# Three summed pairs instead of two in each gate/up block of a hybrid decoder layer

## The chip, the cores and the metric

One Trainium2 chip, one core of it. The metric is the device time in microseconds (us) of one execution of the whole layer, as a median of several runs. Engines are named as in the profile: PE is the matrix engine (PEld its weight loads), DVE the vector engine, ACT the scalar engine, POOL GpSimd, SP the engine that issues the weight transfers.

## The reference, cut to what matters

```
h = x + concat(lru, retention)(rmsnorm(x)) @ w_out        # 256 tokens, model width 2048
u = rmsnorm(h, ln2_w)
ff = silu(u @ w_ffn_gate) * (u @ w_ffn_up)                 # 2048 -> 5632, twice
h = h + ff @ w_ffn_down                                    # 5632 -> 2048
out = rmsnorm(h, final_norm_w)
```

All arrays are float32. The change touches the line of `ff`: the two products of the 256x2048 activations with the 2048x5632 gate and up weights.

## The kernel before

Every large product is made of matmuls on numbers split in two: a float32 tile is cast to a shorter format by ACT (`wh`, line 101) and the remainder is a subtraction on DVE (`wl`, line 102). A product of two split operands is three matmuls: high by high, high by low, low by high (lines 664, 665, 666).

The gate and up products run in 11 blocks of 512 columns (`ffn_block`). In a block the two token halves and the two matrices form a 2x2 array of results: c11 and c21 are the gate columns for tokens 0-127 and 128-255, c12 and c22 the up columns. Each result is 128x512 and stays in a PSUM bank of the pool `paux` (4 banks) while the 2048 rows of the weights go by as 8 *pairs* of 128-row tiles (one `Quad` each, numbered 0 to 7). A pair is a 2x2 by 2x2 block product. Most pairs do it with the 8 plain products (`EIGHT`); a *summed* pair does it with 7 (`SEVEN`), a Strassen-like scheme that multiplies sums of operands. The weights' sums t1 to t4 are built on DVE (lines 625, 626, 628, 629) from the raw 128x512 quarters, and then split like any weight; the activations' sums s1 to s4 are built once for all blocks (`Left`, lines 529 to 535). Four of the seven products (p1, p5, p6, p7) accumulate over all summed pairs of a block in four PSUM banks of their own (pool `pmm`, 4 banks); when the last summed pair is done DVE turns them into contributions to c11, c12, c21, c22 (lines 723 to 729), and at the end of the block lines 731 and 733 add these to what `paux` holds. `gated` then makes silu(gate)*up for each token half (lines 707 to 709).

A summed pair loads as two 512 KB transfers like any other, but takes more tiles: b11 is split alone (`bh`, `bl`, 128x512), then t1|t2, t3|t4 and b22|b21 are split as 128x1024 tiles. So it takes three of the four `wh`/`wl` tile pairs in rotation (pool `split`) and four of the five `raw` tiles (two loaded, two `sum`), where a plain pair takes two and two.

When a block is over, its gated result is transposed for the down product: `turn(b)` (lines 711 to 718) makes four 128x128 transposes on PE into a bank of `pmm` (`ft`), which ACT copies out. The turns are deferred by a number of steps, a step being one pair: turn(0) after the next block's pair 0, turn(1) after its pair 1.

The order of instructions on each engine is fixed when the kernel is built, by a scheduler that starts from the program order; on the chip every engine runs its list in that order and waits for what it needs. Down projection blocks (`down_block`) follow the gate/up blocks and use the same pair scheme, with summed pairs 2, 5, 8, 11, 14 of 22.

Of the kernel before, what the change touches and what calls it, by code (L numbers as in the profile page):

```python
# [28 lines left out]

SUMMED = (2, 4)
SUMMED_DOWN = (2, 5, 8, 11, 14)


# [1 line left out]
def tile_hymba_layer(ctx: ExitStack, tc: tile.TileContext, A: dict, out: bass.AP):  # L37
# [21 lines left out]
    def act_tile(name, dt=F32):  # L59
        return apool.tile([P, 512], dt, tag="act", name=nm(name))  # L60
# [7 lines left out]
    def bank(name):  # L68
        return pmm.tile([P, 512], F32, tag="mm", name=nm(name))
# [149 lines left out]
    def defer(steps, f):  # L219
        later.append([steps, f])  # L220
# [321 lines left out]
    def out_post(f, ps):  # L542
# [10 lines left out]
        if f % 2:  # L553
            hh[f // 2] = Left(hf[0], f // 2 in SUMMED)
        sq = sumsq[:, :S] if f == 0 else act_tile("sq")[:, :S]
# [7 lines left out]
    def norm2():  # L563

        ps = bank("rms")
        for t in range(2):
            pe.matmul(ps[:, 2 * t : 2 * t + 2], sumsq[:, t * P : t * P + P], ones[:, 0:2], start=True, stop=True)
        rsqrt_small(r2_tok, ps[:, 0:4:2], 1.0 / D, 2)
        v.tensor_scalar(out=r2_half, in0=r2_tok, scalar1=0.5, scalar2=None, op0=ALU.mult)
        v.tensor_tensor(out=r2_sq, in0=r2_half, in1=r2_tok, op=ALU.mult)  # L570
# [3 lines left out]
    def resid_tok(cb):  # L574
        for t in range(2):
            ps = bank("ht")
            for i in range(4):
                pe.transpose(ps[:, i * P : i * P + P], xs(4 * cb + i)[:, t * P : t * P + P], ident)
            htok[(cb, t)] = xpool.tile([P, 512], F32, tag="xh", name=nm("htok"))
            act.copy(out=htok[(cb, t)], in_=ps)  # L580
# [61 lines left out]
    def block(quads, lefts, post, ps, tail=(), after=None, ordered=False):  # L642


        n = len(quads) - (2 if tail else 0)
        todo = [(i, c, a, b, 0, 512) for i, q in enumerate(quads[:n]) for c, a, b in (SEVEN if q.sums else EIGHT)]
        for c, c0, cw in tail:
            todo += [(n, c, a, b, c0, cw, i) for i in range(n, len(quads)) for o, a, b in EIGHT if o == c[:3]]
        firsts, lasts = {}, {}
        for m, (_, c, *_) in enumerate(todo):  # L650
            firsts.setdefault(c, m)
            lasts[c] = m
        at = [0]

        def step(i):
            def run():
                while at[0] < len(todo) and todo[at[0]][0] == i:
                    m, (_, c, a, b, c0, cw, *q) = at[0], todo[at[0]]
                    if firsts[c] == m:
                        ps[c] = (aux if c in ("c11", "c12", "c21", "c22") else bank)(c)  # L660
                    q = q[0] if q else i
                    (ah, al), (bh, bl) = lefts[q][a], (t[:, c0 : c0 + cw] for t in quads[q].parts[b])
                    p, last = ps[c][:, c0 : c0 + cw], lasts[c] == m
                    pe.matmul(p, ah, bh, start=firsts[c] == m, stop=False)  # L664
                    pe.matmul(p, ah, bl, start=False, stop=False)  # L665
                    pe.matmul(p, al, bh, start=False, stop=last)  # L666
                    if last:
                        post(c)
                    at[0] += 1
                if after:  # L670
                    after(i)

            return run

        for i in range(n):
            program.append(([quads[i]], step(i)))
        if tail:

            def end():
                with tc.manual_schedule(engines={nc.tensor.engine}) if ordered else ExitStack():  # L680
                    step(n)()

            program.append((quads[n:], end))

    def ffn_block(j):
        def after(i):
            if j == 0 and i == SUMMED[-1] + 1:
                norm2()
            if j in (1, 2) and i < 2:
                resid_tok(2 * j - 2 + i)  # L690
            if j == NB - 1 and i == 0:
                load_fw()

        ps = {}
        quads = [Quad(A["w_gu"][j * (KT // 2) + i], i in SUMMED) for i in range(KT // 2)]
        block(quads, hh, ffn_post(j, ps), ps, after=after)

    def ffn_post(j, ps):
        part = {}

        def other(c, name, a, b, op=ALU.subtract):
            part[c] = act_tile(name)
            v.tensor_tensor(out=part[c], in0=a, in1=b, op=op)

        def gated(t):
            g, u, th = part["c21" if t else "c11"], part["c22" if t else "c12"], act_tile("th")
            act.activation(out=th, in_=g, func=AF.Tanh, scale=r2_half[:, t : t + 1])
            v.scalar_tensor_tensor(out=g, in0=th, scalar=1.0, in1=g, op0=ALU.add, op1=ALU.mult)
            v.scalar_tensor_tensor(out=g, in0=u, scalar=r2_sq[:, t : t + 1], in1=g, op0=ALU.mult, op1=ALU.mult)

        def turn(b):
            pt = bank("ft")
            for c in range(2):
                for t, g in enumerate((part["c11"], part["c21"])):
                    o = c * S + t * P
                    pe.transpose(pt[:, o : o + P], g[:, (2 * b + c) * P : (2 * b + c) * P + P], ident)  # L716
            ff[2 * j + b] = act_tile("ff")
            act.copy(out=ff[2 * j + b], in_=pt)

        def post(c):  # L720
            if c == "p1":
                part["c11"] = act_tile("c11")
                act.copy(out=part["c11"], in_=ps[c])
            elif c == "p7":
                n = act_tile("n")
                v.tensor_tensor(out=n, in0=ps["p6"], in1=part["c11"], op=ALU.subtract)
                other("c12", "c12", n, ps["p5"])
                other("c21", "c21", n, ps["p7"])
                other("c22", "c22", part["c21"], ps["p5"])
            elif c in ("c11", "c12", "c22"):  # L730
                v.tensor_tensor(out=part[c], in0=ps[c], in1=part[c], op=ALU.add)
            elif c == "c21":
                v.tensor_tensor(out=part[c], in0=ps[c], in1=part[c], op=ALU.subtract)
            if c == "c12":
                gated(0)
            if c == "c22":
                gated(1)
                defer(2, lambda: turn(0))
                defer(3, lambda: turn(1))

        return post

# [3 lines left out]
    def load_fw():  # L746
        for c in range(4):
            fw[c] = late_tile("fw")
            nc.sync.dma_start(out=fw[c], in_=A["final_norm_w"][c * 512 : c * 512 + 512].partition_broadcast(P))
# [199 lines left out]
    for step, (units, run) in enumerate(program):  # L949
        need += 2 * len(units)  # L950
        while done < min(len(loads), need + AHEAD):
            un, j = loads[done]
# [108 lines left out]
```

## Time and profile before

| what | value |
|---|---|
| median of 3 runs | 1109.3 us (1109.11 to 1110.9) |
| profiled execution | 1109.8 us, of which the span from first to last instruction is 1108.0 us |
| gate/up blocks | from 387.7 us to about 865 us, 43.12 us each where nothing else runs beside them |
| down blocks | from about 865 us to the end |

The profile is of one execution. The page gives busy time by engine, the share of each in 40 slices of the span, and the chain of work that ended last; the trace behind it is asked for instructions in order of time, for groups by line, and for who waited for whom. A duration of a matmul (0.39 us) is longer than the distance at which the next one starts, since matmuls overlap; the same holds for DVE, with a smaller overlap.

### The profile page before, as it was taken

How to read it: one execution, taken by the hardware profiler on the slowest of the kernel's cores; microseconds unless marked ns; L12 is line 12 of the kernel's file. 1: busy time of each engine (PE TensorE's matmuls, PEld its weight loads, DVE VectorE, ACT ScalarE, POOL GpSimd, SP SyncE). 2: the span in 40 equal slices, each digit the busy share in tenths (PEclk: the TensorE clock that was granted, in tenths of full speed). 3: DMA queues.
4: the chain of work that ended last, by engine and by line, in shares of the span. 5: the costliest groups of instructions: out<-in, count | busy, mean ns of one | idle time of the engine just before them, and what ended most of it. 6: DMA issues, size and time to landing. Idle time of an engine off the chain costs nothing.

```text
span 1108.0 us, 15102 instructions
## 1 busy us (share of the span) xinstructions
PE 1096.1 (99%) x5584; PEld 934.8 (84%) x5584; DVE 880.4 (79%) x1233; ACT 617.2 (56%) x830; POOL 57.7 (5%) x64
## 2 busy tenths in 40 slices
PE   9999999999999999999999999999999999999996
PEld 7998888889988988888888888888888888888885
DVE  7797799987766787787877877887887999777774
ACT  7666644468555565554545545545545666554553
POOL 0602230000000000000000000000000000020001
PEclk9999999999999999999999999999999999999998
DMA  9754575554565555645746656556457465646572
GB/s 323 242 190 153 172 251 168 171 182 150 194 217 188 174 182 177 231 131 192 237 143 228 208 172 228 169 195 226 143 201 243 155 206 199 226 161 212 200 240 76
DMA packets 62217, 214.74 MB, mean 194 GB/s; under 512 B 7104, under 2 KB 7488, under 8 KB 62144
## 3 DMA queue, kind: packets, MB, share of 16 engines
q1 hardware_dynamic: 61344, 211.70, 56.8%
q0 software_dynamic: 512, 1.57, 0.4%
q8 instruction: 43, 0.70, 0.3%
q10 hardware_dynamic: 288, 0.52, 0.1%
q14 instruction: 30, 0.25, 0.1%
HBM read 211.67 MB, written 2.10 MB: 193 GB/s over the span
## 4 chain that ended last, share of the span: by engine, by line
PE 95%; DMA 2%; ACT 1%; POOL 1%; DVE 1%; issue 0%; SPq 0%; DVEq 0%; ACTq 0%; POOLq 0%
PE c L665 18%; PE c L664 18%; PE c L666 18%; PE fm L140 10%; PE fm L141 5%; PE fm L146 3%; PE fm L147 3%; PE fm L145 3%; PE p L666 3%; PE p L664 3%; PE p L665 3%; PE tm L157 2%; PE tm L158 2%; PE tm L156 2%; DMA x<-in_x 1%; PE ft L716 1%
## 5 line engine op out<-in xcount | busy, mean ns | idle before, releaser
L102 DVE TENSOR_TENSOR wl<-raw,wh 128x1024 fp32r<-128x1024 f32 (+1 forms) x364 | 437.3, 1214 | 159.4 <-ACT wh L101 157.8
L101 ACT CAST wh<-raw 128x1024 fp32r<-128x1024 f32 (+1 forms) x364 | 371.2, 1032 | 293.2 <-PE c L666 145.2
L665 PE MATMUL c<-wl,ah 128*128 128x512 f32 x848 | 326.5, 391 | 0.0
L666 PE MATMUL c<-wh,al 128*128 128x512 f32 x848 | 325.5, 389 | 0.0
L664 PE MATMUL c<-wh,ah 128*128 128x512 f32 x848 | 286.5, 390 | 0.0
L666 PEld LDWEIGHTS c<-wh,al 128*128 128x128 f32 x848 | 159.3, 188 | 32.6
L665 PEld LDWEIGHTS c<-wl,ah 128*128 128x128 f32 x848 | 159.2, 188 | 32.7
L664 PEld LDWEIGHTS c<-wh,ah 128*128 128x128 f32 x848 | 159.1, 188 | 32.8
L101 ACT CAST wh<-sum 128x1024 fp32r<-128x1024 f32 x64 | 66.9, 1053 | 85.1 <-PE c L666 40.1
L140 PE MATMUL fm<-u,wh 128*128 128x512 f32 x256 | 90.7, 398 | 0.0
L102 DVE TENSOR_TENSOR wl<-sum,wh 128x1024 fp32r<-128x1024 f32 x64 | 76.8, 1219 | 3.1 <-ACT wh L101 2.5
L140 PE MATMUL fm<-y,wh 128*128 128x512 f32 x224 | 78.9, 398 | 0.0
L146 PE MATMUL fm<-u,wh 128*128 128x256 f32 x256 | 72.7, 284 | 0.0
L145 PE MATMUL fm<-u,wh 128*128 128x256 f32 x256 | 72.7, 284 | 0.0
L147 PE MATMUL fm<-u,wl 128*128 128x256 f32 x256 | 72.3, 283 | 0.0
L141 PE MATMUL fm<-u,wl 128*128 128x256 f32 x256 | 71.9, 281 | 0.0
L141 PE MATMUL fm<-y,wl 128*128 128x256 f32 x224 | 62.4, 281 | 0.0
L820 POOL TENSOR_TENSOR htok<-htok,fw 128x512 f32<-128x512 f32 (+1 forms) x7 | 10.9, 1577 | 906.2 <-ACT junk L818 906.2
L140 PEld LDWEIGHTS fm<-u,wh 128*128 128x128 f32 x256 | 48.1, 188 | 11.6
L140 PEld LDWEIGHTS fm<-y,wh 128*128 128x128 f32 x224 | 41.9, 188 | 10.2
L146 PEld LDWEIGHTS fm<-u,wh 128*128 128x128 f32 x256 | 49.1, 192 | 0.1
L145 PEld LDWEIGHTS fm<-u,wh 128*128 128x128 f32 x256 | 49.1, 192 | 0.1
(248 smaller groups left out, 1497.6 us busy)
## 6 DMA issues: line engine op xcount, KB each, us to landing
raw<-in_w_gu SPq DMA_DIRECT2D x176, 512.0 KB, 5.0
raw<-in_w_down SPq DMA_DIRECT2D x88, 512.0 KB, 4.5
raw<-in_w_out SPq DMA_DIRECT2D x32, 512.0 KB, 4.3
raw<-in_w_lx SPq DMA_DIRECT2D x16, 512.0 KB, 4.9
raw<-in_w_k SPq DMA_DIRECT2D x16, 512.0 KB, 3.7
raw<-in_w_q SPq DMA_DIRECT2D x16, 512.0 KB, 4.3
raw<-in_w_rg SPq DMA_DIRECT2D x16, 512.0 KB, 3.7
raw<-in_w_lg SPq DMA_DIRECT2D x16, 512.0 KB, 3.6
```

Source lines behind the costliest of these rows:

```text
L101: act.copy(out=dst_h, in_=src)
L102: v.tensor_tensor(out=dst_l, in0=src, in1=dst_h.bitcast(F32), op=ALU.subtract)
L140: pe.matmul(ps, wh, hl, start=first, stop=False)
L141: pe.matmul(ps[:, :S], wl, hl[:, :S], start=False, stop=last)
L145: pe.matmul(ps, wh, hl[:, :S], start=first, stop=False)
L146: pe.matmul(ps, wh, hl[:, S:], start=False, stop=False)
L147: pe.matmul(ps, wl, hl[:, :S], start=False, stop=last)
L156: pe.matmul(ps, ah, wh, start=first, stop=False)
L157: pe.matmul(ps, ah, wl, start=False, stop=False)
L664: pe.matmul(p, ah, bh, start=firsts[c] == m, stop=False)
L665: pe.matmul(p, ah, bl, start=False, stop=False)
L666: pe.matmul(p, al, bh, start=False, stop=last)
```

## The change

The first line gives three summed pairs (1, 3, 5) in each gate/up block in place of two (2, 4). The second keeps `norm2` (the second norm's factors, in block 0 alone) where it was, after pair 5. The third puts turn(1) behind pair 0 of the next block, beside turn(0): the four banks of `pmm` are taken by p1, p5, p6, p7 from pair 1 on.

```
-SUMMED = (2, 4)
+SUMMED = (1, 3, 5)
...
-            if j == 0 and i == SUMMED[-1] + 1:
+            if j == 0 and i == SUMMED[-1]:
                 norm2()
...
                 gated(1)
                 defer(2, lambda: turn(0))
-                defer(3, lambda: turn(1))
+                defer(2, lambda: turn(1))
```

What this does to the lists of instructions is shown at three places. A number at the end of a name tells tiles of one kind apart; the two kernels number them differently.

**The end of a block.** First DVE, from the first of the four additions that end a block (L731 and L733) to the first `gated` result (L709 on c11, written 1252 here and 1297 below). Before:

```order
L731 TENSOR_TENSOR c_1252_6383<-c_1204_6189,c_1252_6383 128x512
L733 TENSOR_TENSOR c_1255_6398<-c_1205_6196,c_1255_6398 128x512
L625 TENSOR_TENSOR sum_6580<-raw_6537 128x512
L731 TENSOR_TENSOR c_1254_6396<-c_1206_6203,c_1254_6396 128x512
L708 SCALAR_TENSOR_TENSOR c_1252_6383<-th_6516,c_1252_6383 128x512
L626 TENSOR_TENSOR sum_6580<-sum_6580,raw_6578 128x512
L708 SCALAR_TENSOR_TENSOR c_1255_6398<-th_6527,c_1255_6398 128x512
L731 TENSOR_TENSOR c_1256_6400<-c_1207_6210,c_1256_6400 128x512
L102 TENSOR_TENSOR bl_6540<-raw_6537,bh_6539 128x512
L709 SCALAR_TENSOR_TENSOR c_1252_6383<-c_1254_6396,r_sq,c_1252_6383 128x512
```

With the change, at the same place:

```order
L731 TENSOR_TENSOR c_1297_6494<-c_1243_6267,c_1297_6494 128x512
L733 TENSOR_TENSOR c_1300_6509<-c_1244_6274,c_1300_6509 128x512
L731 TENSOR_TENSOR c_1299_6507<-c_1245_6281,c_1299_6507 128x512
L731 TENSOR_TENSOR c_1301_6511<-c_1246_6288,c_1301_6511 128x512
L102 TENSOR_TENSOR wl_6613<-sum_6608,wh_6612 128x1024
L102 TENSOR_TENSOR wl_6619<-sum_6609,wh_6618 128x1024
L708 SCALAR_TENSOR_TENSOR c_1297_6494<-th_6591,c_1297_6494 128x512
L708 SCALAR_TENSOR_TENSOR c_1300_6509<-th_6602,c_1300_6509 128x512
L709 SCALAR_TENSOR_TENSOR c_1297_6494<-c_1299_6507,r_sq,c_1297_6494 128x512
L709 SCALAR_TENSOR_TENSOR c_1300_6509<-c_1301_6511,r_sq,c_1300_6509 128x512
```

Two 128x1024 subtractions for the next block's summed pair 1 now stand between the last addition (c22) and the first L709. The transposes that wait for these L709 results stand on PE. Before, the second and third of three groups (the first, two transposes, stands 21 matmuls earlier):

```order
L665 MATMUL c_1206_6203<-wl_6180,ah_3629 128x512
L666 MATMUL c_1206_6203<-wh_6179,al_3630 128x512
L716 MATMUL ft_6217<-ident,c_1176_6044 128x128
L716 MATMUL ft_6217<-ident,c_1173_6029 128x128
L716 MATMUL ft_6217<-ident,c_1176_6044 128x128
L665 MATMUL c_1207_6210<-wl_6180,ah_3629 128x512
L666 MATMUL c_1207_6210<-wh_6179,al_3630 128x512
L716 MATMUL ft_6274<-ident,c_1176_6044 128x128
L716 MATMUL ft_6274<-ident,c_1173_6029 128x128
L716 MATMUL ft_6274<-ident,c_1176_6044 128x128
```

With the change there are two groups; the first stands eight matmuls ahead of the second, and the second holds six:

```order
L664 MATMUL c_1243_6267<-wh_6257,ah_3629 128x512
L664 MATMUL c_1245_6281<-wh_6257,sh_3638 128x512
L716 MATMUL ft_6295<-ident,c_1215_6144 128x128
L716 MATMUL ft_6295<-ident,c_1212_6129 128x128
L716 MATMUL ft_6295<-ident,c_1215_6144 128x128
L716 MATMUL ft_6302<-ident,c_1215_6144 128x128
L716 MATMUL ft_6302<-ident,c_1212_6129 128x128
L716 MATMUL ft_6302<-ident,c_1215_6144 128x128
L664 MATMUL c_1244_6274<-wh_6263,ah_3749 128x512
L664 MATMUL c_1246_6288<-wh_6263,ah_3749 128x512
```

**Ahead of pair 5.** DVE again, in the middle of a block. Before, pair 5 is a plain pair and its two subtractions stand behind pair 4's:

```order
L102 TENSOR_TENSOR wl_6638<-raw_6635,wh_6637 128x1024
L102 TENSOR_TENSOR wl_6679<-sum_6674,wh_6678 128x1024
L102 TENSOR_TENSOR wl_6685<-sum_6675,wh_6684 128x1024
L102 TENSOR_TENSOR wl_6689<-raw_6672,wh_6688 128x1024
L102 TENSOR_TENSOR wl_6695<-raw_6692,wh_6694 128x1024
L726 TENSOR_TENSOR n_6748<-p_1311_6655,c_1331_6737 128x512
L102 TENSOR_TENSOR wl_6725<-raw_6722,wh_6724 128x1024
```

With the change pair 3's three subtractions are followed by pair 5's sums, the first of which (L625) stands ahead of pair 4's first subtraction (`wl_6734`):

```order
L102 TENSOR_TENSOR wl_6718<-sum_6713,wh_6717 128x1024
L102 TENSOR_TENSOR wl_6724<-sum_6714,wh_6723 128x1024
L102 TENSOR_TENSOR wl_6728<-raw_6711,wh_6727 128x1024
L625 TENSOR_TENSOR sum_6796<-raw_6767 128x512
L102 TENSOR_TENSOR wl_6734<-raw_6731,wh_6733 128x1024
L102 TENSOR_TENSOR bl_6770<-raw_6767,bh_6769 128x512
L626 TENSOR_TENSOR sum_6796<-sum_6796,raw_6794 128x512
L628 TENSOR_TENSOR sum_6797<-raw_6767,raw_6794 128x512
L102 TENSOR_TENSOR wl_6764<-raw_6761,wh_6763 128x1024
```

So an addition that waits for a transfer (raw_6767) now has a weight tile of the pair before it queued behind it.

**The start of the first block.** PE, at the passage from pair 0 to pair 1 of block 0. Before, the 21st to 30th matmul of the block:

```order
L666 MATMUL c_797_4384<-wh_4217,al_3519 128x512
L664 MATMUL c_797_4384<-wh_4278,ah_3518 128x512
L665 MATMUL c_797_4384<-wl_4279,ah_3518 128x512
L666 MATMUL c_797_4384<-wh_4278,al_3519 128x512
L664 MATMUL c_794_4363<-wh_4284,ah_3629 128x512
L664 MATMUL c_795_4370<-wh_4284,ah_3629 128x512
L664 MATMUL c_796_4377<-wh_4284,ah_3629 128x512
L664 MATMUL c_797_4384<-wh_4284,ah_3629 128x512
L665 MATMUL c_794_4363<-wl_4285,ah_3629 128x512
L666 MATMUL c_794_4363<-wh_4284,al_3630 128x512
```

With the change, the 21st to 30th:

```order
L666 MATMUL c_806_4407<-wh_4226,al_3519 128x512
L664 MATMUL c_806_4407<-wh_4287,ah_3518 128x512
L665 MATMUL c_806_4407<-wl_4288,ah_3518 128x512
L666 MATMUL c_806_4407<-wh_4287,al_3519 128x512
L664 MATMUL c_804_4393<-wh_4372,ah_3629 128x512
L665 MATMUL c_804_4393<-wl_4373,ah_3629 128x512
L666 MATMUL c_804_4393<-wh_4372,al_3630 128x512
L664 MATMUL c_803_4386<-wh_4376,ah_3629 128x512
L664 MATMUL c_805_4400<-wh_4376,sh_3638 128x512
L665 MATMUL c_803_4386<-wl_4377,ah_3629 128x512
```

Pair 1 now needs its second and third tile (wh_4372, wh_4376 with its low part wl_4377) within nine matmuls of pair 0's first tile (wh_4226) being used for the last time, where it needed one tile before.

## The prediction

> **What bounds the kernel now.** I read the page first: the busy time by engine, the clock, and the chain that ended last.
>
> ```profile
> span 1108.0 us, 15102 instructions
> PE 1096.1 (99%) x5584; PEld 934.8 (84%) x5584; DVE 880.4 (79%) x1233; ACT 617.2 (56%) x830; POOL 57.7 (5%) x64
> PEclk9999999999999999999999999999999999999998
> PE 95%; DMA 2%; ACT 1%; POOL 1%; DVE 1%; issue 0%; SPq 0%; DVEq 0%; ACTq 0%; POOLq 0%
> ```
>
> PE is busy for 99% of the span at full clock, and the chain is PE for 95%. So a matmul taken off PE is time taken off, as long as what feeds PE keeps up; DVE with 79% is the next engine. Both are averages, so I read the gate/up stage by itself: PE in order of time (start, duration), from two blocks that follow one another.
>
> ```profile
> 569.76 0.38 PE L716 MATMUL ft<-ident,c 128*128 128x128 f32 x2
> ...
> 603.13 0.39 PE L664 MATMUL c<-wh,ah 128*128 128x512 f32 x1
> ...
> 606.31 0.39 PE L666 MATMUL c<-wh,al 128*128 128x512 f32 x1
> ...
> 610.39 0.39 PE L666 MATMUL c<-wh,al 128*128 128x512 f32 x1
> ...
> 612.88 0.38 PE L716 MATMUL ft<-ident,c 128*128 128x128 f32 x2
> 613.02 0.48 PE L664 MATMUL p<-bh,ah 128*128 128x512 f32 x1
> 613.33 0.40 PE L665 MATMUL p<-bl,ah 128*128 128x512 f32 x1
> ```
>
> From 603.13 to 610.39 there are 32 starts: **0.2269 us per matmul**, not the 0.39 that one lasts. A block takes 612.88 - 569.76 = 43.12 us. It has 2 summed pairs of 7 products and 6 of 8, 62 products or 186 matmuls: 186 x 0.2269 = 42.20. The other 0.92 is the eight transposes. Nothing is left over, so PE doesn't wait in this stage, and a block is set by its count of matmuls.
>
> **How full the others are.** The stretches give busy time in 43 us (PE, PEld, DVE, ACT, then clock and DMA share): one from the middle of the stage, one at the passage to the down blocks.
>
> ```profile
> 560.00:603.00 43.00, 43.00 (x195) 35.56 (x194) 34.27 (x41) 22.62 (x25) 0.00 (x0) 1.00 0.59 196
> 862.00:905.00 43.00, 43.00 (x195) 35.55 (x194) 42.27 (x64) 28.33 (x37) 0.00 (x0) 1.00 0.50 173
> ```
>
> The second row matters most: with DVE busy for 42.27 of 43 us PE was still busy throughout. A nearly full DVE alone has not stopped PE here. What DVE waits for, in the eight blocks from 515 to 860 us (total, times, longest):
>
> ```profile
> ACT wh L101 <- PE c L666: 120.7, 66, 3.8
> DVE wl L102 <- ACT wh L101: 56.7, 32, 3.5
> DVE sum L625 <- DMA raw<-in_w_gu: 11.6, 8, 2.4
> ```
>
> DVE waits for ACT's casts, and these for PE to release a weight tile: the feeders are ahead of PE and held back by it. That is slack, not a limit. Only the third row is a real wait of the feeders: once in each block an L625 waits for its transfer, 1.45 us on average.
>
> **The change, removed.** A third summed pair is one product less per block: 3 matmuls x 11 blocks = 33, x 0.2269 = **7.49 us** off PE. No wait is taken away; PE's own work is. The eight transposes remain; in two groups instead of three they save or cost less than 0.1 us a block (a group of any size ends in one 0.31 us start, 613.02 to 613.33, against 0.23), which I take as nothing.
>
> **Added on DVE.** Per block four sums and one subtraction of 128x512, and one more subtraction of 128x1024. Their starts, in order of time:
>
> ```profile
> 604.58 0.68 DVE L733 TENSOR_TENSOR c<-c,c 128x512 f32<-128x512 f32 x1
> 605.18 0.68 DVE L625 TENSOR_TENSOR sum<-raw 128x512 f32<-128x512 f32 x1
> ...
> 609.38 0.74 DVE L709 SCALAR_TENSOR_TENSOR c<-c,r_sq,c 128x512 f32<-128x512 f32 x1
> 610.04 2.35 DVE L102 TENSOR_TENSOR wl<-raw,wh 128x1024 fp32r<-128x1024 f32 x2
> 612.31 0.74 DVE L709 SCALAR_TENSOR_TENSOR c<-c,r_sq,c 128x512 f32<-128x512 f32 x1
> ...
> 620.07 0.69 DVE L625 TENSOR_TENSOR sum<-raw 128x512 f32<-128x512 f32 x1 [1.19 <-DMA raw<-in_w_gu]
> 620.67 1.22 DVE L102 TENSOR_TENSOR wl<-raw,wh 128x1024 fp32r<-128x1024 f32 x1
> 621.81 0.68 DVE L626 TENSOR_TENSOR sum<-sum,raw 128x512 f32<-128x512 f32 x1
> ```
>
> A 128x512 costs 0.60 (604.58 to 605.18), a 128x1024 1.14 (620.67 to 621.81). So 5 x 0.60 + 1.14 = 4.14 us, and DVE goes from 34.3 of 43.1 to 38.4 of 42.4: 91%, with 4.0 us left in place of 8.8. That is below what the passage to the down blocks shows with PE busy, so the sum lies beside PE and costs nothing. ACT gets one 128x512 cast and one 128x1024 cast more, whose rows are
>
> ```profile
> L101 ACT CAST wh<-raw 128x1024 fp32r<-128x1024 f32 x348 | 361.5, 1051 | 290.2 <-PE c L666 145.2 <-PE fm L140 46.5 <-issue 35.7
> L101 ACT CAST bh<-raw 128x512 fp32r<-128x512 f32 x40 | 24.2, 615 | 13.7 <-DMA raw<-in_w_down 12.2 <-DMA raw<-in_w_gu 1.4
> L718 ACT COPY ff<-ft 128x512 f32<-128x512 f32 x22 | 12.8, 584 | 11.6 <-PE ft L716 11.6
> ```
>
> 1.05 + 0.62 = 1.67 us on an engine with 22.6 of 43 busy: hidden. The transfers stay 16 a block. One more set of activation sums is made once, in the w_out stage: nothing.
>
> A full stretch is not yet an order that fits, so I follow the three places of the listing.
>
> **The end of a block.** The first transpose waits for L709 on c11. Before, the last matmul of c22 starts at 606.31 and the first transpose at 612.88, and that L709 is done at 609.38 + 0.74 = 610.12: 2.8 us to spare. With the change the transposes start 28 matmuls (6.35 us) after c22's last one. DVE does in that time: 0.45 until the matmul has ended, the c22 addition (0.60), two subtractions (2 x 1.14), two L708 (2 x 0.60), L709 (0.74): 5.27. **1.1 us to spare**: no stall. If the cover went, each 0.1 us short would cost 1.1 us over the blocks. Then p6, the first product to need the transposes' banks, comes 6.4 us behind the first transpose; the group of six ends 2.9 in, and the copy takes 0.58: nearly 3 us to spare.
>
> **Ahead of pair 5.** L625 needs a raw tile whose transfer can start only when DVE has done t1|t2 of pair 3 and freed a buffer; pair 4's first subtraction stands behind it. From issue to landing:
>
> ```profile
> raw<-in_w_gu SPq DMA_DIRECT2D x176, 512.0 KB, 5.0
> ```
>
> So pair 4's first low part is ready 5.0 + 0.60 + 1.22 = 6.8 us after t1|t2 of pair 3. On PE the first uses of the two lie 19 matmuls apart, 4.3 us. So it fits if t1|t2 of pair 3 is 2.5 us ahead of PE. It should take the weight tile that PE uses for the last time 26 matmuls ahead, 5.90 us; less the end of that matmul, the cast and the subtraction (0.39 + 1.05 + 1.22 = 2.66, and some 0.1 for signals) it is 3.1 ahead. **0.6 us to spare**, the tightest place. A transfer as early as the median costs nothing, the one end. For the other, the longest wait of the L625 row, 2.4 us, is 0.95 longer than its mean: a transfer that late would stop PE by 0.35 us, 3.9 us if in every block (and by 0.7 us a block more if the tile is the one freed three matmuls later). I take nothing, since the median is the nearest row, and keep 3.9.
>
> **The start of block 0.** The block starts at this row:
>
> ```profile
> 387.67 0.40 PE L664 MATMUL c<-wh,ah 128*128 128x512 f32 x1
> ```
>
> Pair 1's third tile needs a weight buffer, and the first one freed is that of pair 0's first tile, last used by the 21st matmul: 20 x 0.2269 + 0.39 = 4.93 us in. Cast and subtraction take it to 7.2; PE wants the low part with the 30th matmul, 6.6 us in. **0.7 us of stall, once.** With a buffer freed earlier it would be nothing, with that of pair 0's second tile (last used by the 24th matmul, 0.7 later) 1.4. I take 0.7, between the two.
>
> **Sum.** -7.49 + 0.7 = -6.8 us. The profiled execution's 1109.8 us (span 1108.0 and 1.8 around it) would become 1103.0; it lies 0.5 above the median of the runs, so from 1109.3 the forecast is **1102.5 us**.
>
> **Rivals.** *A, late transfers:* the place ahead of pair 5 gives way. For it: the L625 row above shows one such wait in each block now, and there will be two that follow a summed pair. Against: PE does not start late in any block now. Price: up to 3.9 us, so 1102.5 to 1106.4; at half of it 1104.5.
>
> *B, DVE becomes the bound, slower than before:* its waits don't shrink to fit. They are now (56.7 + 11.6) / 8 = 8.5 us per block, with 4.0 us of room. Up to 4.7 us of waiting (43.12 - 38.4) the block is no longer than before; from there it is slower. If 6 us stayed, since a summed pair's three tiles of two products each pass through four buffers faster than a plain pair's, a block would take 44.4 and the kernel 1109.3 + 11 x 1.3 = 1123 us. Against it: the stretch from 862 with 0.7 us of waiting left.
>
> *C, no overlap on a full DVE:* by the rows' durations in place of their starts, a block of the change has 19 subtractions of 1.22, 23 operations of 0.68 and two each of 0.68 and 0.74 on DVE: 41.7 us. With two transfer waits of 1.45 it is 44.6, 1.5 over 43.12, so 1126 us. Against: two subtractions of 1.22 took 2.35 together, and the next one started 2.27 after the first (610.04 to 612.31). The Trainium skill, VectorE: DVE Perf Modes, "The DRAIN you can't avoid", says that the next op does not start until the pipeline is empty, which would be this case; the starts of this trace speak against it, by 0.08 us an instruction.
>
> *D, the banks:* p5 to p7 of pair 1 need two banks that the transposes have just held. If ACT's copies came 3 us later than reckoned and PE waited 0.7 us per block, the 7.5 us would be gone: about 1109. ACT is half idle, so it is unlikely. That the change doesn't do what it says is not open: the listing has the matmuls fewer and the turns together.
>
> **How the numbers follow.** Forecast (0 to 0.2 us of stall per block, 1101.5 to 1104): 0.66. A: 0.19. B: 0.07. C: 0.02. D: 0.06. The range leaves out B to D (0.15) and 0.02 of A, the later tile, above, and about 0.03 below. It goes from 1101.0, which is no stall at all (1101.8) and 0.8 us for the spread of the runs, to 1107.0, all of A and 0.6. A measurement of this kernel can tell about 0.2% (2.2 us; its three runs spread by 1.8) from no change, so faster means below 1107.1: forecast and most of A, 0.83. D and A with the later tile give same 0.08; B and C slower 0.09.
>
> **What would show it.** Right: 33 matmuls fewer, a block from transpose to transpose of 42.4 us, no PE wait on DVE or ACT, and DVE at 38 of 42.4 with its wait for ACT's casts down to half. Wrong at the end of a block: PE ft waiting for DVE L709. Wrong ahead of pair 5: PE c L665 waiting for DVE wl, with DVE sum L625 waiting for DMA just before, more than 2 us. At the start: one PE wait for wl near 394 us. B shows as PE waits all over the block with DVE still waiting for ACT. D shows as PE p waiting for ACT ff. A mistake in the count of 0.2269 would show as a block that is longer with no wait.

## The result, and the profile after

| | median, us | lowest to highest, us |
|---|---|---|
| before | 1109.11 (5 runs) | 1108.89 to 1110.9 |
| after | 1120.75 (5 runs) | 1119.21 to 1121.52 |

The ratio is 1.0101, with a 95% interval of 1.0089 to 1.0112. The change makes the kernel 11.6 us slower; 1102.5 was forecast, with 1107.0 as the upper end. The page of after, whose lines answer to those shown of before:

```profile
span 1119.0 us, 15134 instructions
PE 1093.3 (98%) x5551; PEld 928.9 (83%) x5551; DVE 927.3 (83%) x1304; ACT 632.9 (57%) x853; POOL 58.4 (5%) x64
PE 77%; DVE 9%; DMA 8%; ACT 2%; issue 2%; POOL 1%; SPq 0%; DVEq 0%; ACTq 0%; POOLq 0%
L664 PE MATMUL c<-wh,ah 128*128 128x512 f32 x782 | 260.1, 393 | 13.0 <-DVE c L731 13.0
L625 DVE TENSOR_TENSOR sum<-raw 128x512 f32<-128x512 f32 x43 | 29.6, 689 | 42.2 <-DMA raw<-in_w_gu 40.0
```

The matmuls are 33 fewer (5551 for 5584), as forecast. But the chain that ended last was 95% PE and is now 77%, with 9% DVE and 8% transfers. The fourth line names a wait that before did not have: 13.0 us in which PE stood ahead of a `c` matmul (L664) until an addition L731 on DVE was done. The fifth: DVE's first sum of a summed pair waited 40.0 us for its transfer.

The waits of PE (total, times, longest) show that it is ten waits, one for each block start after the first (the start of the down blocks hardly waits), and nearly all of PE's waiting:

```profile
PE c L664 <- DVE c L731: 13.0, 10, 2.0
PE warm L94 <- DVE eps_t L87: 1.0, 1, 1.0
PE rms L250 <- POOL sumsq L290: 0.8, 1, 0.8
PE p L664 <- ACT bh L101: 0.7, 1, 0.7
```

**Where the time went.** I take as gate/up stage the time from the first matmul of block 0 to that of the down blocks; before it runs from 387.67 (in the prediction's listing) to the first row here, after from the second to the third:

```profile
865.29 0.39 PE L664 MATMUL c<-wh,ah 128*128 128x512 f32 x1
```
```profile
386.93 0.40 PE L664 MATMUL c<-wh,ah 128*128 128x512 f32 x1
...
875.12 0.47 PE L664 MATMUL c<-wh,ah 128*128 128x512 f32 x1
```

So 477.62 us became 488.19: +10.6, of a span that grew by 11.0. With 7.5 us of matmuls less, 18.1 us were lost there. From start to start on PE, less the usual 0.2269, the ten block starts lose 14.4, block 0 loses 0.8 more than before, and a drop of the clock behind one of the waits 1.5 (last section). The remaining 1.4 is many gaps under 0.12 us.

**What happens at a block start.** First PE at the end of a block of after, then DVE at the same place (start, duration, and in brackets the idle time with what ended it):

```profile
649.30 0.39 PE L666 MATMUL c<-wh,al 128*128 128x512 f32 x1
...
653.38 0.39 PE L666 MATMUL c<-wh,al 128*128 128x512 f32 x1
655.49 0.47 PE L664 MATMUL c<-wh,ah 128*128 128x512 f32 x1 [1.72 <-DVE c L731]
```
```profile
646.77 0.68 DVE L703 TENSOR_TENSOR c<-c,p 128x512 f32<-128x512 f32 x1
649.37 0.69 DVE L625 TENSOR_TENSOR sum<-raw 128x512 f32<-128x512 f32 x1 [1.91 <-DMA raw<-in_w_gu]
649.98 1.22 DVE L102 TENSOR_TENSOR wl<-raw,wh 128x1024 fp32r<-128x1024 f32 x1
651.11 0.68 DVE L102 TENSOR_TENSOR bl<-raw,bh 128x512 fp32r<-128x512 f32 x1
651.71 0.69 DVE L626 TENSOR_TENSOR sum<-sum,raw 128x512 f32<-128x512 f32 x1
652.32 1.22 DVE L102 TENSOR_TENSOR wl<-raw,wh 128x1024 fp32r<-128x1024 f32 x1
653.45 0.69 DVE L628 TENSOR_TENSOR sum<-raw,raw 128x512 f32<-128x512 f32 x1
654.05 0.69 DVE L629 TENSOR_TENSOR sum<-sum,raw 128x512 f32<-128x512 f32 x1
654.65 0.69 DVE L731 TENSOR_TENSOR c<-c,c 128x512 f32<-128x512 f32 x1
```

The last matmul on c11 starts at 649.30, 18 matmuls ahead of the block's end at 653.38. From 649.7 on, DVE could add c11 and free its PSUM bank. It does so only at 654.65, since seven instructions for pairs 0 and 1 of the *next* block (five of them pair 1's) stand ahead of that addition in its list, and the first of them, L625, waited 1.91 us for its transfer. The next block's first product goes into the freed bank, so PE starts at 655.49 in place of 653.61: 1.88 us late, as long as the wait for the transfer. From the end of its wait DVE worked without a stop for 5.28 us (649.37 to 654.65); with no wait it would have been just in time, with nothing to spare. At the second and third of the ten starts the wait is one step further back: DVE waits for ACT's cast of b11 (`bh`), and that cast for its transfer. The Trainium skill (TensorE: Matmul & The Clock Gate, "Architectural detail: the array is 16× 32×32, not 1× 128×128") says that DVE's queue is strictly first in, first out; these rows agree: an addition whose operands had been ready for 5 us stood behind one that waited for data.

**Why the transfer is late.** Throughput of the transfers in the 28 us ahead of that place, 40 slices of 0.7 us:

```profile
GB/s 0 53 246 404 117 281 375 100 176 293 252 310 199 164 41 0 0 0 0 88 357 380 328 316 275 293 339 351 228 199 181 222 222 369 386 421 322 252 310 164
```

From 632 to 635 us hardly anything moves: pair 5 holds four of the five raw buffers. Then the transfers are made up for in one stretch, close to one another. Issue to landing (the last number, us) of the first in that stretch, of one within it, and of the one for which the L625 above waits (issued at 634.68, 639.94 and 643.42):

```profile
raw<-in_w_gu SPq DMA_DIRECT2D x1, 512.0 KB, 3.1
...
raw<-in_w_gu SPq DMA_DIRECT2D x1, 512.0 KB, 6.5
...
raw<-in_w_gu SPq DMA_DIRECT2D x1, 512.0 KB, 5.5
```

Such a hole is not the harm by itself. Before has one of 6 us (649.4 to 655.5), and its transfer queue waits about as long for summed pairs to give back their first raw tile (for L628, from 480 to 870 us: 69.9 us, against 73.8 in after). So these rows suggest why the transfer is late; whether the held buffers are the reason is for the experiments to show.

So theory T: *a summed pair holds four raw buffers; with three such pairs the transfers behind them are late, and DVE's list passes the lateness on to PE, because the addition that frees c11's bank stands behind the sum that waits.* The main rival D: *DVE has too much work*. Its busy time in after is as forecast (38.0 to 38.5 us) but the blocks are 44 us long:

```profile
617.00:661.00 44.00, 42.28 (x191) 34.73 (x190) 38.04 (x46) 23.58 (x28) 0.00 (x0) 1.00 0.56 189
661.00:705.00 44.00, 42.69 (x192) 35.03 (x191) 38.45 (x47) 23.83 (x28) 0.00 (x0) 1.00 0.56 192
```

### The profile page after: what moved, and what is told of

It is laid out like the page before. It is cut to its first block, busy times and chain, and to the rows that moved or that the text cites. A ratio compares the mean times of both kernels' runs of the same rounds, so it can differ in the third digit from the quotient of the medians.

```text
span 1119.0 us, 15134 instructions
## 1 busy us (share of the span) xinstructions
PE 1093.3 (98%) x5551; PEld 928.9 (83%) x5551; DVE 927.3 (83%) x1304; ACT 632.9 (57%) x853; POOL 58.4 (5%) x64
## 4 chain that ended last, share of the span: by engine, by line
PE 77%; DVE 9%; DMA 8%; ACT 2%; issue 2%; POOL 1%; SPq 0%; DVEq 0%; ACTq 0%; POOLq 0%
PE c L664 13%; PE c L666 12%; PE c L665 12%; PE fm L140 10%; DMA raw<-in_w_gu 6%; PE fm L141 5%; DVE wl L102 4%; PE p L664 3%; PE p L666 3%; PE p L665 3%; PE fm L146 3%; PE fm L147 3%; PE fm L145 3%; PE tm L156 2%; PE tm L158 2%; PE tm L157 2%
## 5 line engine op out<-in xcount | busy, mean ns | idle before, releaser
L101 ACT CAST wh<-raw 128x1024 fp32r<-128x1024 f32 (+1 forms) x353 | 360.5, 1030 | 254.1 <-issue 69.9
L665 PE MATMUL c<-wl,ah 128*128 128x512 f32 x782 | 301.9, 391 | 0.5 <-DVE wl L102 0.5
L666 PE MATMUL c<-wh,al 128*128 128x512 f32 x782 | 301.5, 390 | 0.0
L664 PE MATMUL c<-wh,ah 128*128 128x512 f32 x782 | 260.1, 393 | 13.0 <-DVE c L731 13.0
L664 PEld LDWEIGHTS c<-wh,ah 128*128 128x128 f32 x782 | 146.5, 188 | 46.7 <-issue 9.6
L666 PEld LDWEIGHTS c<-wh,al 128*128 128x128 f32 x782 | 147.2, 188 | 30.5
L101 ACT CAST wh<-sum 128x1024 fp32r<-128x1024 f32 x86 | 88.6, 1050 | 106.6 <-DVE sum L626 39.4
L102 DVE TENSOR_TENSOR wl<-sum,wh 128x1024 fp32r<-128x1024 f32 x86 | 103.0, 1223 | 12.9 <-ACT wh L101 12.2
L625 DVE TENSOR_TENSOR sum<-raw 128x512 f32<-128x512 f32 x43 | 29.6, 689 | 42.2 <-DMA raw<-in_w_gu 40.0
L140 PEld LDWEIGHTS fm<-u,wh 128*128 128x128 f32 x256 | 48.1, 188 | 11.7
L101 ACT CAST bh<-raw 128x512 fp32r<-128x512 f32 x51 | 31.4, 622 | 42.7 <-DMA raw<-in_w_gu 34.4
```

What stands on the lines that cost most here:

```text
L101: act.copy(out=dst_h, in_=src)
L102: v.tensor_tensor(out=dst_l, in0=src, in1=dst_h.bitcast(F32), op=ALU.subtract)
L140: pe.matmul(ps, wh, hl, start=first, stop=False)
L625: v.tensor_tensor(out=t1, in0=b11, in1=b12, op=ALU.add)
```

## The experiments

The kernels of one set ran on one chip, with the kernel before beside them (1109.2 to 1109.7 us). "Stage" is the gate/up stage as defined above, "down" the time from its end to the end of the last matmul; both are of one profiled execution. (The expectations below put "down" 0.1 to 0.2 us higher.)

| run | time, us | ratio, 95% interval | stage | down |
|---|---|---|---|---|
| before | 1109.1 | | 477.6 | 233.8 |
| after | 1120.8 | 1.0089 to 1.0112 | 488.2 | 234.9 |
| e1: six raw buffers | 1114.7 | 1.0034 to 1.0064 | 477.3 | 239.0 |
| e2: order on DVE | 1115.6 | 1.0039 to 1.0069 | 482.6 | 235.0 |
| e3: before, turns moved | 1109.0 | 0.9984 to 1.0003 | 477.5 | 233.8 |
| e4: pairs 1, 3 | 1109.9 | 0.9995 to 1.0014 | 479.8 | 234.8 |
| e5: pairs 2, 4, 6 | 1128.7 | 1.0153 to 1.0200 | 495.9 | 235.0 |
| e6: before, DVE work bunched | 1115.3 | 1.0033 to 1.0066 | 484.1 | 233.9 |
| e7: one own sum buffer | 1112.2 | 1.0020 to 1.0043 | 481.4 | 235.7 |
| e8: e7 and order | 1110.6 | 1.0000 to 1.0019 | 477.3 | 234.8 |
| e9: two own sum buffers and order | 1110.4 | 1.0002 to 1.0020 | 476.9 | 235.6 |
| e10: two own sum buffers | 1121.4 | 1.0095 to 1.0122 | 486.4 | 235.9 |
| e11: before, DVE work spread | 1110.7 | 1.0003 to 1.0021 | 478.9 | 233.9 |
| e12: pairs 2, 4, 6, two own | 1110.3 | 0.9997 to 1.0016 | 475.4 | 237.1 |
| e13: e12 in gate/up only | 1108.4 | 0.9983 to 1.0000 | 475.2 | 234.9 |
| e14: e9 in gate/up only | 1109.3 | 0.9990 to 1.0008 | 476.5 | 234.6 |
| e16: pairs 2, 4, two own | 1112.1 | 1.0013 to 1.0031 | 479.5 | 233.9 |

**e1, a raw buffer more.** The list on DVE at a block's end keeps L625 and the other sums ahead of the c11 addition.

```
-    apool = ctx.enter_context(tc.tile_pool(name="acts", bufs=58))
+    apool = ctx.enter_context(tc.tile_pool(name="acts", bufs=57))
...
-    rpool = ctx.enter_context(tc.tile_pool(name="raw", bufs=5))
+    rpool = ctx.enter_context(tc.tile_pool(name="raw", bufs=6))
```

> The changed kernel (1120.8 us) with six raw buffers in place of five, and one activation buffer less (57 for 58) to make room. Theory T (late transfers in line ahead of the bank): a summed pair holds four of the five raw buffers, so the transfers behind it start late, the first sum of the next block's pair 1 (L625) waits for its transfer on DVE, the addition L731 on c11 stands behind it, and PE waits at the block's start for the PSUM bank. With a sixth buffer the transfers start earlier: L625 waits less than 0.5 us there, the ten PE waits for L731 (15.0 us in all, with the clock drop behind one) go, and the time is 1103 to 1108 us. Rival D (DVE is simply too full at 38 of 42.4 us): the work on DVE is unchanged, so 1118 to 1122 us. Rival W (the four weight tiles are the limit): unchanged too, 1118 to 1122.

Measured 1114.7 us. DVE at a block's end, where the same seven instructions stand ahead of L731 as in after, in another order:

```profile
642.05 0.69 DVE L102 TENSOR_TENSOR bl<-raw,bh 128x512 fp32r<-128x512 f32 x1
642.66 0.69 DVE L625 TENSOR_TENSOR sum<-raw 128x512 f32<-128x512 f32 x1
...
647.34 0.68 DVE L731 TENSOR_TENSOR c<-c,c 128x512 f32<-128x512 f32 x1
```

L625 doesn't wait here (elsewhere it still does, 16.9 us in all), and PE loses at most 0.15 us at a block's start; its one wait for the addition that is left, 1.3 us, is at the start of the down blocks. The stage is back at 477.3 us with the same work on DVE. So the late transfers are a cause. The total missed T's range: the down stage took 5.1 us more than before (e1 gives up an activation buffer there; that this is the reason was not shown), and blocks still take 42.8 to 43.3 us where 42.4 would be free of waits.

**e2, the order on DVE alone.** Raw buffers as in after.

```
+            with tc.issue_after(self.behind) if self.behind else ExitStack():
+                if self.late:
+                    self.first()
...
+                ins = v.tensor_tensor(out=part[c], in0=ps[c], in1=part[c], op=ALU.add)
+                if c == "c11" and j + 1 < NB:
+                    blocks[j + 1][SUMMED[0]].behind = ins.ins
```

The block of `issue_after` holds t1 and t3 of pair 1 and (`first`) its b11 split: on DVE they come behind the instruction named.

> The changed kernel with five raw buffers as it has, but in blocks 1 to 10 the sums and the b11 split of pair 1 are put on DVE behind the addition L731 on c11 of the block before. Theory T: PE's wait at the block's start goes although the transfer lands no earlier: 15 us off, 1104 to 1109 us; L625 still waits for its transfer, up to 2 us. Rival F (the transfers themselves are too late whatever the order): the wait turns up a pair later, PE waiting for wl of pair 1, and the time stays at 1115 us or more. Rival D (DVE too full): 1118 to 1122 us.

1115.6 us: the waits for the c11 addition are gone from the block starts (one of 0.8 us is left, at the start of the down blocks). About half of the loss in the stage goes (482.6), and T's range is missed. The rest is spread over waits for `wh`, `wl` and `bh` in summed pairs, none above 1.1 us: rival F, in part. DVE still waits for the transfers (L633 and L634 are t1 and t3 here), and now also 0.8 us a block for the last matmul on c11, ahead of the sums that have been put behind that addition:

```profile
DVE sum L633 <- DMA raw<-in_w_gu: 18.2, 21, 2.9
DVE sum L634 <- DMA raw<-in_w_gu: 10.9, 10, 1.4
```

**e3, the turns alone, and e4, two pairs at 1 and 3.** e3 is before with `defer(2, lambda: turn(1))`; e4 is after with `SUMMED = (1, 3)`.

> The kernel before (summed pairs 2 and 4) with only the second turn moved beside the first. Theory T and rival D: no cost, 1108.5 to 1110.5 us. Rival M (the move of the turn costs PE or the banks something): 1112 us or more.

> The changed kernel with two summed pairs, 1 and 3, in place of three; the second norm's factors stay behind pair 5. PE has the matmuls of the kernel before and DVE too; only the places differ. Theory T: after pair 3 five plain pairs let the transfers catch up before the next pair 1, so L625 waits little at the block's end and the time is that of before with the one stall in block 0: 1109 to 1111 us. Rival P (a summed pair as second pair of a block is itself the trouble, with the additions behind its sums): PE still waits 1 us or more at the block starts, 1116 us or more. Rival D: 1109 to 1111 us.

Both at before's time. The move of the turn costs nothing. A summed pair as the second of a block, with its sums ahead of the c11 addition as in after, costs two waits (1.4 and 0.8 us) in ten block starts when five plain pairs lie ahead of it. Both stand behind a b11 cast on ACT that had waited for its transfer (3.2 and 2.6 us): here the order hurts where a transfer is late as well.

**e5, pairs 2, 4, 6.** After with `SUMMED = (2, 4, 6)` and the second turn behind pair 1 again.

> Summed pairs 2, 4 and 6 in place of 1, 3 and 5, and the second turn behind pair 1 again as before; PE and DVE have exactly the changed kernel's work, and five raw buffers are held as often. Only the place differs: here the addition on c11 stands ahead of the first sum of the next summed pair on DVE. Theory T (a late transfer in line ahead of the bank costs, the work does not): the PE waits for the c11 addition at block starts fall from 13 to under 4 us and the time is 1105 to 1113 us, as the two runs that took one of the two away gave 1115. Rival D (38 us of DVE work in a 42.4 us block can't be fed): 1117 to 1122 us, wherever the pairs lie.

1128.7 us: both missed. T was right in one part, the waits for the c11 addition are 3.7 us; but it had taken the line on DVE for the whole way from late transfers to PE. Here L625 waits in three places of a block for up to 5.9 us, and what queues behind it are weight tiles:

```profile
684.23 0.69 DVE L625 TENSOR_TENSOR sum<-raw 128x512 f32<-128x512 f32 x1 [5.94 <-DMA raw<-in_w_gu]
...
686.08 2.35 DVE L102 TENSOR_TENSOR wl<-raw,wh 128x1024 fp32r<-128x1024 f32 x2
```

**e6 and e11, the work on DVE alone.** Before with seven additions of 128x512 more per block; in e11 each is held behind a subtraction of a plain pair.

```
+                v.tensor_tensor(out=extra, in0=sumsq, in1=sumsq, op=ALU.add)
```

> The kernel before with seven additions of 128x512 more on DVE in each gate/up block (their result is used by nothing): 7 x 0.60 = 4.2 us, the work that the third pair adds, with no transfer, raw buffer, cast or matmul changed. Rival D (DVE too full): DVE at 38.5 of 43.1 us stalls PE as in the changed kernel, block 44 us, 1116 us or more. Theory T (the late transfers and the raw buffers): 1109 to 1111.5 us. Between the two, 1112 to 1115, the DVE work pays a part.

> The kernel before with seven additions of 128x512 more per block on DVE, now each queued behind a subtraction of a plain pair so that they lie spread (in the first such run the scheduler had put all 77 into the first five blocks, 10 us in each, and those blocks grew by 2 us). DVE at 38.5 of 43.1 us, as in the changed kernel. Rival D (that much work stalls PE): 1113 us or more. Theory T: a fifth of the wait of the earlier run at most, 1109 to 1110.8 us.

e6 did not do what its text says: the scheduler put all 77 additions into the first five blocks, some 15 in each. It shows what a full DVE costs: two of these blocks take 1.0 us longer than before's, the next two, at 43.3 to 43.6 us busy of 45, 2.0 to 2.4 us. e11 has the amount that the third pair adds, in every block; the first two lines are of e6, the others of e11:

```profile
533.00:578.00 45.00, 43.68 (x193) 34.97 (x192) 43.27 (x56) 22.18 (x25) 0.00 (x0) 1.00 0.56 183
578.00:623.00 45.00, 44.03 (x195) 35.20 (x194) 43.60 (x57) 22.29 (x26) 0.00 (x0) 1.00 0.58 191
```
```profile
528.00:571.00 43.00, 43.00 (x196) 35.61 (x195) 38.62 (x48) 22.61 (x26) 0.00 (x0) 1.00 0.59 195
571.00:614.00 43.00, 43.00 (x195) 35.64 (x194) 38.62 (x48) 22.61 (x26) 0.00 (x0) 1.00 0.59 195
```

With DVE busy for 38.62 of 43 us PE was busy for all of it. That is the DVE load of after without its transfers and without its order, so the amount of work alone is not the cause, and rival D falls in that form. The 1.4 us more than before are one gap of 1.5 at the passage to the down blocks.

**e7 to e10, sum tiles out of the raw pool.** e7 gives t3|t4 a buffer of its own (a pool `sums` in room that is free in this stage), e9 and e10 both sum tiles; e8 and e9 have the order of e2 as well.

```
-            ta, tb = (rpool.tile(...) for _ in range(2))
+            ta, tb = (late[1].tile(..., tag="sum") for _ in range(2))
```

> The changed kernel where the tile of t3|t4 has a buffer of its own (in room that is free in this stage) in place of one of the five raw buffers, with all 58 activation buffers kept. So a summed pair holds three raw buffers, not four. Theory T: as with six raw buffers the waits for the c11 addition go (under 3 us of 13); the 4 us that the run with six raw buffers lost in the down blocks, put down to the activation buffer that it gave up, are not lost here: 1108 to 1112 us. Rival B (the raw buffer is not what mattered, the activation buffer or the order was): 1115 us or more.

> Both remedies together: t3|t4 in a buffer of its own, and pair 1's sums behind the c11 addition on DVE. Theory T (both late transfers and the line on DVE): what is left of waits in the gate/up blocks, 0.4 to 1.5 us a block in the two single remedies, falls below 0.3; 1103 to 1108 us, faster than before. Rival R (a third cause remains: with 4 us of room, DVE hands weight tiles over too late at other places): no better than the better of the two single remedies, 1110 us or more.

> The changed kernel with both sum tiles (t1|t2 and t3|t4) in two buffers of their own, so that a summed pair holds two raw buffers like a plain pair, and with pair 1's sums behind the c11 addition. Room comes from tables that are used only before the gate/up stage, so no activation buffer is given up. Theory T (transfers late because summed pairs hold the raw buffers, passed on by DVE's order): with one sum tile moved out the blocks were at 43.3 us; now L625 and bh wait less than 3 us in all for transfers, blocks of 42.5 to 42.8 us, 1103 to 1107 us, faster than before. Rival D (DVE work): blocks stay at 43.3, 1109 to 1112 us.

> The same two buffers, without the order put by hand (L625 of the next pair 1 may stand ahead of the c11 addition). Theory T, transfers alone: once they are early the line on DVE is harmless, and the time is within 2 us of the run with the order, 1104 to 1109 us. If the order matters by itself (DVE reaches L731 late because of the work queued ahead of it), PE still waits for the c11 addition about 0.5 us a block, as with one buffer, and the time is 1109 to 1113.

e7 came out 0.2 us above T's range, and PE still waited 5.6 us for the c11 addition where T had under 3. e8 and e9 missed T's ranges; they are at about before's time, 10 us better than after but not faster than before: rival R is right as to the total. (e9's time lies in the range given for D as well, but e11 excludes D's reason.) In e9 the blocks in mid-stage are at 42.8 to 43.5 us. PE stops for 0.25 in nearly each block for the t3|t4 tile of pair 1, whose cast on ACT waits for the last sum on DVE:

```profile
653.31 1.05 ACT L102 CAST wh<-sum 128x1024 fp32r<-128x1024 f32 x1 [1.35 <-DVE sum L642]
```

The sums that were put behind the c11 addition are now a little late themselves: the order takes one wait away and leaves a smaller one.

e10 missed by 8 us. Its DVE waits less for transfers than after's (20.9 us against 40.0), and yet it is as slow. Its edit differs from e9's only by the order on DVE, and that is worth 11.0 us: 9.5 in the stage, of which PE loses 6.7 at the block starts. At one of these starts (the c11 addition is L736 there) DVE's first sum waited 0.76 us for its transfer; then DVE worked without a stop through the same seven instructions and came to the addition at 652.18, half a microsecond too late for PE:

```profile
646.90 0.69 DVE L630 TENSOR_TENSOR sum<-raw 128x512 f32<-128x512 f32 x1 [0.76 <-DMA raw<-in_w_gu]
...
651.58 0.69 DVE L634 TENSOR_TENSOR sum<-sum,raw 128x512 f32<-128x512 f32 x1
652.18 0.69 DVE L736 TENSOR_TENSOR c<-c,c 128x512 f32<-128x512 f32 x1
```

So this does not show that the order costs by itself: without the 0.76 us DVE would have been in time. The same holds for every start at which e10's PE was late (nine of ten, by 0.1 to 1.8 us): ahead of each, DVE's sums waited longer for transfers than PE lost. With buffers of their own for the sums the transfers come earlier than in after, but not early enough for this order; the transfer of the row above was issued at 643.3, when a subtraction on DVE had freed its raw buffer, and landed 3.6 us later.

The same count tells why e1 was spared. From the first of the seven instructions to the addition it takes 5.3 us in after, e10 and e1 alike (649.37 to 654.65, 646.90 to 652.18, 642.05 to 647.34). In after the first one starts 0.1 us behind the last matmul on c11, in e10 1.3 us ahead of that matmul (648.21), in e1 1.9 us ahead (643.98), and PE is late by 1.9, 0.5 and 0 us.

**e12 to e14 and e16, the other places, with buffers.** e12 is e5 with the two own sum buffers; e13 has them in the gate/up blocks alone, e14 the same for e9. e16 is the control, before with these buffers in the gate/up blocks.

> Summed pairs 2, 4, 6 (1128.7 us with five raw buffers for all) with the two sum tiles in buffers of their own. Theory T: that kernel's waits of L625 for transfers (52 us in all, up to 5.9 each) are the cause of its time; with early transfers they fall under 10 us and the time to 1104 to 1112 us. Rival P (the place in the block costs by itself, since p5 to p7 are worked off only one pair before the block's end): 1118 us or more.

> Summed pairs 2, 4, 6 with the two sum tiles in buffers of their own, but only in the gate/up blocks; the down blocks take their sum tiles from the raw pool again as in the kernel before. In the run with own buffers for both, the gate/up stage took 475.4 us (2.2 less than before) and the down stage 237.3 (3.3 more). Theory T with the loss in the down blocks put down to their own sum buffers: the stage stays at 475 to 476, the down stage falls back to 234 to 235, and the time is 1106 to 1108.5 us, faster than before. Rival L (the down stage loses because the gate/up stage hands over differently): down stage 236 or more, 1109 to 1111 us.

> Summed pairs 1, 3, 5 with the two own buffers in the gate/up blocks alone and pair 1's sums behind the c11 addition. With own buffers for both stages the gate/up stage took 476.9 us and the down stage 235.7, where before has 477.6 and 233.9. Theory T: down stage back to 234 to 235 and 1108 to 1110 us. Rival L: 1110 to 1111.5.

> The kernel before (summed pairs 2 and 4) with the same two sum buffers in the gate/up blocks: the control for the other two. Its PE does not wait in that stage, so the buffers can bring nothing there: theory T says 1108.5 to 1110.5 us. Rival B (the buffers or the moved tables bring or cost something by themselves): more than 2 us off 1109.3 either way.

e12 is 18 us faster than e5, and rival P falls: at pairs 2, 4, 6 the sum tiles in the raw pool were the cause (the room for their own buffers moves some tables, and the scheduler may shift a few rows with it; that was not tested apart). DVE's wait of its first sum for a transfer, of e5 and of e12 (L630 there), falls by two thirds, though not below the 10 us expected:

```profile
DVE sum L625 <- DMA raw<-in_w_gu: 52.3, 22, 5.9
```
```profile
DVE sum L630 <- DMA raw<-in_w_gu: 16.9, 13, 1.9
```

Six of e12's blocks take 42.8 us: here the saving of the third pair shows. PE still starts most blocks in mid-stage 0.27 us late: DVE comes late to the c11 addition, after it had waited 1.5 us for products of pair 6, which is rival P's mechanism at a small price. It was lost in the down blocks (237.1 us), which used the own buffers too; e13 takes them back there, gets 234.9, and with 1108.4 us is the best kernel of the study. Its ratio to before, 0.9983 to 1.0000, is too small to be told from no change; against after it is 12 us, against its control e16 3.7 us. e16 missed: with two pairs the buffers cost 2.8 us (rival B). That after, e2, e4, e5, e13 and e14 need 0.7 to 1.2 us more in the down blocks than before does, where nothing is changed, fits a weaker form of rival L (its 236 us were not reached); it was not followed further.

## Why the prediction was wrong

- **The matmuls: right.** 33 fewer, at 0.227 us. A block of e13 without a wait, from first matmul to first matmul:

```profile
519.77 0.39 PE L669 MATMUL c<-wh,ah 128*128 128x512 f32 x1
...
562.23 0.47 PE L669 MATMUL c<-wh,ah 128*128 128x512 f32 x1
```

  42.46 us, where 42.4 was forecast. What was taken off PE was worth what the text says; it was given back as waits.
- **"The sum lies beside PE and costs nothing": right as work** (38 us busy, and e11), **wrong as order.** It asked whether DVE has room in a block. It did not ask what the added instructions stand in front of.
- **"The end of a block" is the step that failed.** It followed one chain, c22's last matmul to L709 to the transposes, and that chain held: PE waited for no transpose. But the step put PE's stall there at nothing, with 1.1 us to spare, and PE lost 14.4 us at the ten block starts, 0.3 to 2.1 us each. It left out the four additions themselves. Each frees a PSUM bank that the next block's products go into, c11's first of all. In the old list c11's addition stood ahead of the next summed pair's sums, in the new one behind them, so a late transfer in front of a sum became a late bank; the listing of the change began at the first addition and so cut off just what had come to stand in front of it.
- **"Ahead of pair 5": the right kind of wait at the wrong place.** L625 does wait there now, up to 3.1 us (at 675.99). But 2.4 us was taken as the longest lateness of a transfer, from a trace in which a summed pair held the raw buffers twice a block. The price of 3.9 us in all was set by that, and the same wait at the block's end was not priced at all. Ahead of pair 5 itself PE did not stop even at 3.1 us: the room there was larger than the 0.6 us reckoned.
- **The start of block 0: right.** One wait for `wl` at 394.33, 0.70 us from start to start.
- **ACT, the banks (D), the missing overlap on DVE (C): right**, none shows. The rule that C names goes on in the same paragraph of the Trainium skill (VectorE: DVE Perf Modes, "The DRAIN you can't avoid"): a next operation that is not held starts earlier. The trace agrees, with starts 0.60 us apart at 0.68 us each.
- **Rival B had the outcome, by luck.** It said that about 6 us of DVE's waits would stay and a block take 44.4 us, 1123 in all; DVE stands idle for 5.5 to 6 us of each 44. It was given 0.07, and for a reason, the four weight tiles, that no run bears out: e1 and e12 have the same four. Its sign did not show either: PE's waits lie at the block starts and not all over the block, and DVE's wait for ACT's casts fell from 81.9 to 17.4 us (from 380 to 880 us of the span). The reasons shown are late transfers, which more buffers relieve (e1, e12), and the order that passes them on (e2, e9 against e10). Why the transfers are still late with the sums in buffers of their own (20.9 us of such waits in e10) stays open; even e13's stage gains only 2.4 of the 7.5 us, and late block starts take 4.3 of the rest.

## What to carry to other kernels

When work is added to an in-order engine, list what stands behind each added instruction that can wait for a transfer, up to the next one that frees something for the bottleneck (a PSUM bank, a weight tile); spare busy time says nothing about it. Count how many buffers of a pool each step holds and for how long: tiles made from loaded tiles, when they come from the loading pool, close it for transfers, and the transfers that then start together each take longer. Here the stage became shorter than before's by more than 2 us only in e12 and e13, where the place and the buffers took care of both, and after that the next waits (0.3 us a block, and the passages between stages) ate most of the gain.

## What the hardware did that was not expected

After one of the ten waits PE's clock fell. The windows ahead of the fall and in it (the value behind the busy times is the granted clock), and PE's starts:

```profile
562.50:565.91 3.41, 1.48 (x7) 0.93 (x7) 3.41 (x6) 2.06 (x3) 0.00 (x0) 1.00 0.39 120
565.91:569.32 3.41, 3.41 (x10) 2.63 (x9) 3.41 (x5) 1.27 (x3) 0.00 (x0) 0.50 0.49 190
```
```profile
565.53 0.47 PE L664 MATMUL c<-wh,ah 128*128 128x512 f32 x1 [1.93 <-DVE c L731]
...
568.33 0.63 PE L665 MATMUL c<-wl,ah 128*128 128x512 f32 x1
568.76 0.63 PE L666 MATMUL c<-wh,al 128*128 128x512 f32 x1
```

For eight matmuls the starts lie 0.43 us apart in place of 0.23, which costs 1.5 us on top of the wait. From 565.91 to 569.32, for 3.41 us, the granted clock was 0.50. The Trainium skill (TensorE: Matmul & The Clock Gate, Part 1, "What's actually happening") gives the half clock as the state after at least one idle window of about 3.4 us; here PE had been busy for 1.48 of the 3.41 us ahead of the drop, with the wait of 1.93 us as its longest pause. The Trainium skill (TensorE: Matmul & The Clock Gate, Part 1, "Wait — 56ns, not 53.3ns?") states 426.7 ns from start to start at half clock for 512 columns, which these starts agree with. A wait of 1.96 us at 788.22 was followed by no drop, so the length alone does not decide it; what does, no run here shows.
